# Attention probabilities turned by VectorE and DRAM instead of TensorE, with value products 7 units behind the scores

## The chip, the cores and the metric

One core of one Trainium2 chip runs the whole program. The metric is device time in microseconds for one execution. The engines named below are TensorE (PE, with its weight loads PEld), VectorE (DVE), ScalarE (ACT), GpSimd (POOL) and SyncE (SP, which here only issues transfers). Each engine works through its own list of instructions in order and waits on semaphores. Sixteen DMA engines carry the transfers that SP, GpSimd or ScalarE issue.

## The reference

The reference is one layer of a transformer trunk on 512 tokens of width 2048, all in float32: sliding-window attention, its output projection, a gated embedding and a last norm. What matters here is the attention.

```python
q, k, v, gate = jnp.split(h @ w_in, [...])          # 32 query heads, 4 key and value heads, 64 wide
scores = einsum('bnqhgd,bnjhd->bnhgqj', q, kb) * 64 ** -0.5 + bias   # window of 128 keys, bias by distance
m = maximum(scores.max(-1), sink)
e = exp(scores - m)
probs = e / (e.sum(-1) + exp(sink - m))
out = einsum('bnhgqj,bnjhd->bnqhgd', probs, vb)
return (out * silu(gate)) @ w_out
```

Each query sees itself and the 127 tokens before it. Softmax runs along the keys, and the product with the values sums over the keys. A matmul sums over partitions, so the probabilities, which come out of softmax with queries on the partitions and keys along the row, must be turned before that product.

## The kernel before

**Precision.** A float32 number is split into a high part in the fast float32r format and the rest. A product is three matmuls, high by high, low by high and high by low (`mm3`, lines 123 to 128, so most TensorE time in the profile stands on lines 126 to 128). Each weight tile of 128 x 1024 is loaded (line 102, SP), copied to its high part by ScalarE (line 109) and its low part is made by VectorE (line 110). Three raw buffers go round: a load waits until the tile three before it has been split.

**Stages.** First the norm and the first projections (to about 74 us). Then the attention stage: 30 column blocks of queries (`qps`) and gates (`gps`) are still to be projected, 16 groups of `mm3` each, and the attention's small products go in between. Then the output projection, and then the gated embedding, which ends with the store. The two last stages use a scheme that multiplies sums of weight blocks. Those sums are made in DRAM during the attention stage: SP issues copies (line 723) and GpSimd issues transfers that add a second block (line 725). Each copy and each add is 512 KB, 64 of each, paced by `sums_in`.

**Units.** The attention has 64 units: 8 groups of four heads (`TWOS`, index `d`) by 8 stretches of 64 queries (`UNITS`, index `g`). A unit has 2 x 128 rows: 4 heads by 32 queries, twice. `scores(i)` issues the score products (line 485), bias additions and the maximum on VectorE (lines 513 to 525), the exponential on ScalarE (line 529), the reciprocal of the sum (line 531), and the scaling by it into a tile `pr` (line 542). Where a unit lies at an odd place, the two halves of its keys are swapped on the way, so that rows of keys line up with the values.

`turn(i)` turns `pr` on TensorE by a product with the identity (line 551, into a PSUM bank `pt`), and ScalarE and VectorE split the result into high and low (lines 564 and 565; a group's first unit, `g == 0`, has only 64 keys and its own form, lines 558 to 562). From `g == 2` on, GpSimd selects a triangle of the result into `own` (line 575), and ScalarE copies the upper or the lower half of that (line 585). `weigh(i)` makes the products with the values (lines 601 to 605), and each second unit adds both halves into `U` (lines 614 to 616, with two temporary tiles). Later `gate_value` (line 630) multiplies `U` by the gate, which frees the `U` tile.

**Order.** TensorE, SP, VectorE, ScalarE and GpSimd keep the program's order in this stage; no planner changes it. The loop at lines 936 to 973 writes that order: iteration `i` issues the first part of `scores(i)`, `turn(i - 2)` and `weigh(i - 3)`, then some 7 groups of the projection, with the rest of the small work placed between the groups by their number `n` (`some(W.todo)` makes the next weight tile, `chores` and `idle` hold evacuations of the projections and gates). It has 67 iterations, and `left // (blocks + 2 - i)` deals out the groups. `q_at` (line 181) fixes which of the 30 column blocks are queries, so that each group of heads has its queries in time.

**A turn by DRAM that is there already.** Between the output projection and the next stage, `turn_blocks` (lines 1062 to 1075) has VectorE turn 32 x 32 blocks, GpSimd store them to DRAM and gather them back (lines 1077 to 1083) with the blocks in their turned places.

Of the kernel before, what the change touches and what calls it, by code (L numbers as in the profile page):

```python
# [11 lines left out]
F32 = mybir.dt.float32  # L12
# [7 lines left out]
S = 512  # L20
P = 128
# [5 lines left out]
PAIRS = HEADS // 2  # L27
# [28 lines left out]
def trunk_kernel(ctx: ExitStack, tc: tile.TileContext, a: dict):  # L56
# [292 lines left out]
    for part in (first_q[0][0], first_q[1][0], *first_q[0][1:], *first_q[1][1:]):  # L349
        part()  # L350

    kt = [kvq.tile([P, S], F32, name=f"kt{t}") for t in range(2)]
    K = {}

    def make_key(h):
# [113 lines left out]
    def scores(i):  # L469

        d, g = divmod(i, UNITS)
        if g == 4 and d + 1 < TWOS:
            load_bias(d + 1)
        of_keys = K[d // 2].rearrange("p j l k -> p (j l k)")

        s_ps = spsum.tile([P, 2, S], F32, tag="w", name=f"s{i}")  # L480
        number = [min(2 * g + u + 1, 5) * QB for u in range(2)]
        for u in range(2):
            first, n = max(2 * g + u - 4, 0), number[u]
            st = Q[d][:, 2 * g + u].rearrange("p h q -> p (h q)")
# [24 lines left out]
        bias = biases[d][:, ::-1]  # L509
        if g < 2:  # L510
            for u, n in enumerate(number):
                blocks_of, high, low = by_block(t[:, u, 1 : 1 + n], u, n)
                nc.vector.tensor_add(blocks_of, high, bias[:, KEYS - n :].rearrange("p (j k) -> p j k", k=QB))
            for u, n in enumerate(number):
                blocks_of, high, low = by_block(t[:, u, 1 : 1 + n], u, n)
                nc.vector.tensor_add(blocks_of, low, blocks_of)
        else:
            x = t[:, :, 1 : 1 + KEYS].rearrange("p u (j k) -> p u j k", k=QB)
            of = s_ps[:, :, : 2 * KEYS].rearrange("p u (j l k) -> p u l j k", l=2, k=QB)
            spread = bias.rearrange("p (j k) -> p j k", k=QB).unsqueeze(1).to_broadcast([P, 2, KEYS // QB, QB])  # L520
            nc.vector.tensor_add(x, of[:, :, 0], spread)
            nc.vector.tensor_add(x, of[:, :, 1], x)
# [12 lines left out]
        for u in range(2):  # L535
            out, src = T[i][:, u], pr[u]
            if g == 0:
                out = T[i][:, 0, u * HB : (u + 1) * HB]
            if late and (g + u) % 2:
                out = out.rearrange("p (h k) -> p h k", h=2)[:, ::-1]  # L540
                src = src.rearrange("p (h k) -> p h k", h=2)
            nc.scalar.mul(out, src, sm[:, 4 + u : 5 + u])

    def turn(i):


        d, g = divmod(i, UNITS)
        pr = T.pop(i)
        pt = bank(f"pt{i}", "t")[:, :256]
        for u in range(2 if g else 1):  # L550
            nc.tensor.transpose(pt[:, u * P : (u + 1) * P], pr[:, u, :], ident)  # L551

        r = operands.tile([P, 2, 256], F32R, tag="r", name=f"r{i}", bufs=2)
        rh, rl = (r[:, l].rearrange("p (h u q) -> p u h q", h=4, u=2) for l in range(2))
        src = pt.rearrange("p (u h q) -> p u h q", u=2, h=4)
        if g == 0:
            lower, upper = slice(0, HB), slice(HB, P)
            nc.scalar.copy(rh[lower, 0], src[lower, 0])
            nc.scalar.copy(rl[upper, 1], src[upper, 0])
            nc.vector.tensor_sub(rh[upper, 0], src[lower, 0], rh[lower, 0].bitcast(F32))  # L560
            nc.vector.tensor_sub(rh[upper, 1], src[upper, 0], rl[upper, 1].bitcast(F32))
            nc.scalar.copy(rh[lower, 1], rl[upper, 1].bitcast(F32))
        else:
            nc.scalar.copy(rh, src)  # L564
            nc.vector.tensor_sub(rl, src, rh.bitcast(F32))  # L565
        yield
# [20 lines left out]
    def weigh(i):  # L587
# [3 lines left out]
        kv = d // 2  # L591
        r, own = PT.pop(i)
        if g == 0:
            U[d] = apool.tile([P, 2, S], F32, tag="u", name=f"u{d}", bufs=3)
# [14 lines left out]
        if b:  # L609
            dst = U[d][:, :, n * P : (n + 1) * P].rearrange("p u (b q) -> p b u q", b=2)  # L610
            lower, upper = slice(0, 64), slice(64, 128)
            tmp = [apool.tile([P, 2, 2, HB], F32, tag=f"tmp{e}", name=f"tmp{e}_{i}", bufs=1) for e in range(2)]
            for e, (o, x) in enumerate(((lower, upper), (upper, lower))):
                nc.scalar.copy(tmp[e][o], ops[x, :, :, e, :])
            for e, o in enumerate((lower, upper)):
                nc.vector.tensor_add(dst[o], ops[o, :, :, e, :], tmp[e][o])
        if g == UNITS - 1:
            for c in (2 * d, 2 * d + 1):
                weighed.add(c)
# [299 lines left out]
    def sums_in(i):  # L919


        if i == 0:
            return range(0, SUMS_EARLY, 2)
        if i < 4:
            return range(4 * i + 3, min(4 * i + 7, SUMS_EARLY), 2)
        n, of = SUM_STEPS - SUMS_EARLY, blocks - 4
        return range(SUMS_EARLY + (i - 4) * n // of, SUMS_EARLY + (i - 3) * n // of)

    left = KC * (len(kinds) - 1)
# [3 lines left out]
            of.pop(0)()  # L933

    softmax = iter(())
    for i in range(blocks + 3):

        before, softmax = softmax, scores(i) if i < blocks else iter(())
        turned = turn(i - 2) if 2 <= i < blocks + 2 else iter(())
        value = weigh(i - 3) if 3 <= i else iter(())  # L940
        next(turned, None)
        next(value, None)
        next(softmax, None)
        next(turned, None)
        next(before, None)
        next(softmax, None)
        first_chores(i, 0)
        if i in (6, 20, 36):
            idle.extend(make_key(1 + i // 16))
        todo = left // (blocks + 2 - i) if i < blocks + 2 else 0  # L950
        left -= todo
        for n in range(max(todo, 6)):
            if n < todo:
                next(proj)
            if n == 0:
                first_chores(i, 1)
                some(W.todo)
                some(chores or idle)
            elif n == 2:
                next(turned, None)  # L960
                next(value, None)
                if len(chores) > 1:
                    some(chores)
            elif n == 3:
                next(softmax, None)
            elif n == 4:
                first_chores(i, 2)
                some(chores or idle)
            elif n == 5:
                next(softmax, None)  # L970
        if i < blocks:
            for n in sums_in(i):
                sum_weights(n)
    for _ in proj:
# [863 lines left out]
```

## Time and profile before

| | |
|---|---|
| Median of 3 runs | 781.91 us (781.47 to 781.96) |
| Profiled execution | 781.41 us, span 779.7 us |
| TensorE busy | 770.1 us, 99% of the span |
| VectorE busy | 618.9 us, 79% |
| ScalarE busy | 529.3 us, 68% |
| GpSimd busy | 169.8 us, 22% |
| DMA | 217.22 MB, mean 279 GB/s |
| Granted TensorE clock | 0.997 |

The page gives the busy time of each engine and its share of the span, then the span in 40 equal slices, where each digit is a share in tenths. The queues q1 and q0 are the transfers issued by SP and those issued by GpSimd. A group of instructions is a line of the kernel, an engine, an operation, the tiles it writes and reads, a shape and a count, then the total busy time and the mean of one in ns, and then the idle time before them with what ended it. In a table of stretches each row has the stretch, its length, the busy time and number of instructions of each engine, the granted clock, the share of time in which the DMA engines were busy, and the GB/s that they moved. That share is a sum over packets, and can pass 1 where two packets overlap on an engine.

### The profile page before, as it was taken

Reading aid. Unit: us, or ns where it says so; the run is one execution under the profiler, and the core shown is the slowest. Engines: PE = TensorE matmul, PEld = TensorE weight load, DVE = VectorE, ACT = ScalarE, POOL = GpSimd, SP = SyncE. Lnnn points to the kernel's source line nnn. Section 1 sums busy time; section 2 is a strip of 40 time slices with the busy share of each in tenths; the row PEclk is TensorE's granted clock in tenths of the full one; section 3 lists DMA queues with packets and bytes.
Section 4 is the critical chain, followed back from the end, with each engine's and each line's share of the span. In section 5 each row is a group of like instructions: output and inputs, shape, how many; then the busy total and the mean of one; then the engine's idle time right before and its main releaser. Section 6 shows DMA issues by size and latency. Waiting matters only on the chain.

```text
span 779.7 us, 11154 instructions
## 1 busy us (share of the span) xinstructions
PE 770.1 (99%) x3652; PEld 644.1 (83%) x3652; DVE 618.9 (79%) x1069; ACT 529.3 (68%) x1121; POOL 169.8 (22%) x307
## 2 busy tenths in 40 slices
PE   9999999999999999999999999999999999999995
PEld 8888888888888888888888888888888888888884
DVE  4546697876978688777877799968799889999995
ACT  6743586766777676766766664577766888867874
POOL 0201523132232313132332200112101122221111
PEclk9999999999999999999999999999999999999998
DMA  9978899999999999999998588999899999999956
GB/s 343 305 207 301 182 260 311 272 312 258 287 247 278 280 241 278 277 279 277 248 288 218 136 298 313 359 290 290 318 389 337 320 284 295 325 264 309 321 132 216
DMA packets 52858, 217.22 MB, mean 279 GB/s; under 512 B 8112, under 2 KB 9136, under 8 KB 46720
## 3 DMA queue, kind: packets, MB, share of 16 engines
q1 hardware_dynamic: 39280, 156.67, 56.5%
q0 software_dynamic: 13520, 59.83, 36.2%
q8 instruction: 29, 0.48, 0.3%
q14 instruction: 29, 0.24, 0.1%
HBM read 199.65 MB, written 82.89 MB: 362 GB/s over the span
## 4 chain that ended last, share of the span: by engine, by line
PE 98%; issue 1%; DVE 0%; POOL 0%; POOLq 0%; DVEq 0%
PE gps L126 7%; PE gps L127 7%; PE gps L128 7%; PE qps L126 7%; PE qps L128 7%; PE qps L127 7%; PE o L126 6%; PE o L127 6%; PE o L128 6%; PE g L127 5%; PE g L128 5%; PE g L126 5%; PE s L485 2%; PE vps L290 2%; PE o L603 2%; PE pt L551 2%
## 5 line engine op out<-in xcount | busy, mean ns | idle before, releaser
L766 DVE TENSOR_TENSOR blo<-braw,bhi 128x1024 fp32r<-128x1024 f32 x100 | 121.5, 1220 | 20.9 <-ACT bhi L765 19.9
L765 ACT CAST bhi<-braw 128x1024 fp32r<-128x1024 f32 x100 | 105.1, 1052 | 47.1 <-PE o L128 15.1
L126 PE MATMUL gps<-xh,whi 128*128 128x512 f32 x256 | 100.0, 390 | 0.0
L127 PE MATMUL gps<-xl,whi 128*128 128x512 f32 x256 | 99.9, 390 | 0.0
L128 PE MATMUL gps<-xh,wlo 128*128 128x512 f32 x256 | 99.8, 390 | 0.0
L126 PE MATMUL qps<-xh,whi 128*128 128x512 f32 x224 | 87.8, 392 | 0.0
L128 PE MATMUL qps<-xh,wlo 128*128 128x512 f32 x224 | 87.5, 390 | 0.0
L127 PE MATMUL qps<-xl,whi 128*128 128x512 f32 x224 | 87.4, 390 | 0.0
L575 POOL TENSOR_SCALAR_AFFINE_SELECT own<-r 64x512 fp32r<-64x512 f32 (+1 forms) x48 | 32.5, 677 | 238.4 <-DVE r L565 234.4
L110 DVE TENSOR_TENSOR wlo<-wraw,whi 128x1024 fp32r<-128x1024 f32 x60 | 73.5, 1227 | 2.8 <-ACT whi L109 2.7
L126 PE MATMUL o<-bhi,fho 128*128 128x512 f32 x192 | 74.8, 390 | 0.0
L127 PE MATMUL o<-blo,fho 128*128 128x512 f32 x192 | 74.7, 389 | 0.0
L128 PE MATMUL o<-bhi,flo 128*128 128x512 f32 x192 | 74.7, 389 | 0.0
L109 ACT CAST whi<-wraw 128x1024 fp32r<-128x1024 f32 x60 | 62.3, 1040 | 4.6 <-issue 4.1
L126 PE MATMUL g<-bhi,fhg 128*128 128x512 f32 x160 | 62.3, 390 | 0.0
L127 PE MATMUL g<-blo,fhg 128*128 128x512 f32 x160 | 62.2, 389 | 0.0
L128 PE MATMUL g<-bhi,flg 128*128 128x512 f32 x160 | 62.2, 389 | 0.0
L128 PEld LDWEIGHTS gps<-xh,wlo 128*128 128x128 f32 x256 | 48.1, 188 | 10.3
L126 PEld LDWEIGHTS gps<-xh,whi 128*128 128x128 f32 x256 | 48.1, 188 | 9.2
L529 ACT ACTIVATE t<-t,sm 128x129 f32<-128x129 f32 (+1 forms) x128 | 49.6, 389 | 8.7 <-DVE sm L525 7.4
L127 PEld LDWEIGHTS gps<-xl,whi 128*128 128x128 f32 x256 | 48.1, 188 | 8.9
L565 DVE TENSOR_TENSOR r<-pt,r 128x256 fp32r<-128x256 f32 x56 | 23.7, 424 | 38.9 <-ACT r L564 38.1
(299 smaller groups left out, 1827.6 us busy)
## 6 DMA issues: line engine op xcount, KB each, us to landing
wraw<-in_w_gate_in SPq DMA_DIRECT2D x32, 512.0 KB, 8.1
w_out<-in_w_out POOLq DMA_DIRECT2D x32, 512.0 KB, 9.1
braw<-w_out SPq DMA_DIRECT2D x32, 512.0 KB, 8.1
wraw<-in_w_q SPq DMA_DIRECT2D x28, 512.0 KB, 6.7
braw<-in_w_out SPq DMA_DIRECT2D x22, 512.0 KB, 5.7
braw<-in_ple_gate SPq DMA_DIRECT2D x22, 512.0 KB, 6.9
ple_gate<-in_ple_gate POOLq DMA_DIRECT2D x20, 512.0 KB, 8.9
xw<-in_first SPq DMA_DIRECT2D x14, 640.5 KB, 6.5
```

Of the source, the lines that this page charges most:

```text
L109: nc.scalar.copy(hi, raw)
L110: nc.vector.tensor_sub(lo, raw, hi.bitcast(F32))
L126: nc.tensor.matmul(ps, sh, mh, start=first, stop=False, skip_group_check=more)
L127: nc.tensor.matmul(ps, sh, ml, start=False, stop=False, skip_group_check=more)
L128: nc.tensor.matmul(ps, sl, mh, start=False, stop=last, skip_group_check=more)
L290: nc.tensor.matmul(v_ps[t], h[:, c], part_of(high_at, 256, 512), start=f, stop=e, skip_group_check=True)
L485: nc.tensor.matmul(s_ps[:, u, : 2 * n], st, of_keys[:, first * 2 * QB : (first * QB + n) * 2], start=True, stop=True)
L529: nc.scalar.activation(su, su, AF.Exp, bias=sm[:, u : u + 1], accum_out=sm[:, 2 + u : 3 + u])
L565: nc.vector.tensor_sub(rl, src, rh.bitcast(F32))
L575: nc.gpsimd.affine_select(out=flat(own), in_=flat(r).bitcast(F32), pattern=[[0, 8], [sign, HB]], compare_op=ALU.is_ge, fill=0.0, base=-HB ...
L765: nc.scalar.copy(hi[:, :n], raw)
L766: nc.vector.tensor_sub(lo[:, :n], raw, hi[:, :n].bitcast(F32))
```

## The change

`turn` no longer uses TensorE. ScalarE scales the probabilities in place. VectorE turns each 32 x 32 block of a unit into one half of a tile `turned`, which holds two units. `send` (issued by ScalarE) stores that tile to DRAM, and `fetch` (four transfers issued by SP, one for each 32 keys) gathers it into a tile `back`, where keys are on the partitions. `turn` splits from `back` instead of from PSUM. A fourth of the pairs begin with a unit of 64 keys, and leave out the unused quarter (`within`).

Iteration `i` now does `scores(i)`, the split of unit `i - 5`, and the value products of unit `i - 7`, in 70 iterations over which the projection's groups are dealt evenly. A pair `a` is stored in iteration `2a + 2` after group 4 and gathered in iteration `2a + 4` after group 2; its first unit is split in iteration `2a + 5` after group 2. The adds into weight sums go on for four iterations more. `q_at` follows the new pace. To make room, `U` has two buffers instead of three, and the seventh `U` lies where the keys were (`both_kt`), and one temporary tile takes the place of two.

```diff
-    q_at = {int(0.5 + 3.516 * (c // 2)) - 3 + c % 2: c for c in range(2, PAIRS)}
+    q_at = {int(0.5 + 3.333 * (c // 2)) - 3 + c % 2: c for c in range(2, PAIRS)}
...
-        T[i] = operands.tile([P, 2, P], F32, tag="pr", name=f"pr{i}", bufs=3)
         for u in range(2):
-            out, src = T[i][:, u], pr[u]
+            nc.scalar.mul(pr[u], pr[u], sm[:, 4 + u : 5 + u])
+        yield
+
+        a, v = divmod(i, 2)
+        if not v:
+            T[a] = operands.tile([P, 512], F32, tag="turned", name=f"turned{a}", bufs=2)
+        to = T[a].rearrange("p (j v u q) -> p v u j q", j=4, v=2, u=2)[:, v]
+        for u in range(2):
+            out, src = to[:, u], pr[u].rearrange("p (j q) -> p j q", q=QB)
             if g == 0:
-                out = T[i][:, 0, u * HB : (u + 1) * HB]
+                out = to[:, 1, 2 * u : 2 * u + 2]
             if late and (g + u) % 2:
...
-            nc.scalar.mul(out, src, sm[:, 4 + u : 5 + u])
+                out = out[:, ::-1]
+            nc.vector.transpose(out, src)
+
+    def within(v, a):
+        return v[:, :, QB if a % (UNITS // 2) == 0 else 0 :]
+
+    def send(a):
+        apart_of[a] = tc.dram_tile([P, 512], F32, name=f"turned_of{a}")
+        nc.scalar.dma_start(*(within(v.rearrange("p (j x) -> p j x", j=4), a) for v in (apart_of[a], T.pop(a))))
+
+    def fetch(a):
+        back[a] = operands.tile([P, 512], F32, tag="back", name=f"back{a}", bufs=2)
+        src = apart_of.pop(a).rearrange("(h k) (j x) -> j k h x", h=4, j=4)
+        for j in range(4):
+            to = back[a][QB * j : QB * j + QB].rearrange("p (h x) -> p h x", h=4)
+            nc.sync.dma_start(within(to, a), within(src[j], a))
 
     def turn(i):
-        pr = T.pop(i)
-        pt = bank(f"pt{i}", "t")[:, :256]
-        for u in range(2 if g else 1):
-            nc.tensor.transpose(pt[:, u * P : (u + 1) * P], pr[:, u, :], ident)
+        src = back[a].rearrange("p (h v x) -> p v h x", h=4, v=2)[:, v]
...
-        n, of = SUM_STEPS - SUMS_EARLY, blocks - 4
+        n, of = SUM_STEPS - SUMS_EARLY, blocks
...
-    for i in range(blocks + 3):
+    total = left
+    turned = iter(())
+    for i in range(blocks + 7):
         before, softmax = softmax, scores(i) if i < blocks else iter(())
-        turned = turn(i - 2) if 2 <= i < blocks + 2 else iter(())
-        value = weigh(i - 3) if 3 <= i else iter(())
-        next(turned, None)
+        value = weigh(i - 7) if 7 <= i else iter(())
         next(value, None)
         next(softmax, None)
         next(turned, None)
         next(before, None)
         next(softmax, None)
...
-        todo = left // (blocks + 2 - i) if i < blocks + 2 else 0
-        left -= todo
-        for n in range(max(todo, 6)):
+        share = total * (i + 1) // (blocks + 6) - total * i // (blocks + 6) if i < blocks + 6 else 0
+        for n in range(max(share, 6)):
...
+            if n == 4 and i % 2 == 0 and 2 <= i <= blocks:
+                send(i // 2 - 1)
+            if n == 2 and i % 2 == 0 and 4 <= i <= blocks + 2:
+                fetch(i // 2 - 2)
+            if n == 2:
+                next(turned, None)
+            if n == 1:
+                next(before, None)
...
+            if n == 2:
+                turned = turn(i - 5) if 5 <= i < blocks + 5 else iter(())
                 next(turned, None)
...
-        if i < blocks:
+        if i < blocks + 4:
             for n in sums_in(i):
                 sum_weights(n)
```

More of the change, by code (lines that the diff above doesn't have):

```diff
@@ L350, in trunk_kernel @@
         part()
-    kt = [kvq.tile([P, S], F32, name=f"kt{t}") for t in range(2)]
+    both_kt = kvq.tile([P, 2, S], F32, name="kt")
+    kt = [both_kt[:, t] for t in range(2)]
     K = {}
@@ L553, in turn @@
+    def turn(i):
+        g = i % UNITS
+        a, v = divmod(i, 2)
+        src = back[a].rearrange("p (h v x) -> p v h x", h=4, v=2)[:, v]
         r = operands.tile([P, 2, 256], F32R, tag="r", name=f"r{i}", bufs=2)
[L554 to L555 removed]
         if g == 0:
+            rh, rl = (r[:, l].rearrange("p (h u q) -> p u h q", h=4, u=2) for l in range(2))
+            src = src[:, :, QB:]
@@ L557, in turn @@
             lower, upper = slice(0, HB), slice(HB, P)
[L558 to L561, printed above, removed]
+            nc.scalar.copy(rh[lower, 0], src[lower])
+            nc.scalar.copy(rl[upper, 1], src[upper])
+            nc.vector.tensor_sub(rh[upper, 0], src[lower], rh[lower, 0].bitcast(F32))
@@ L562, in turn @@
+            nc.vector.tensor_sub(rh[upper, 1], src[upper], rl[upper, 1].bitcast(F32))
             nc.scalar.copy(rh[lower, 1], rl[upper, 1].bitcast(F32))
         else:
+            rh, rl = (r[:, l].rearrange("p (h x) -> p h x", h=4) for l in range(2))
             nc.scalar.copy(rh, src)
@@ L593, in weigh @@
         if g == 0:
-            U[d] = apool.tile([P, 2, S], F32, tag="u", name=f"u{d}", bufs=3)
+            U[d] = both_kt if d == 6 else apool.tile([P, 2, S], F32, tag="u", name=f"u{d}", bufs=2)
         if b == 0:
@@ L611, in weigh @@
             lower, upper = slice(0, 64), slice(64, 128)
-            tmp = [apool.tile([P, 2, 2, HB], F32, tag=f"tmp{e}", name=f"tmp{e}_{i}", bufs=1) for e in range(2)]
+            tmp = apool.tile([P, 2, 2, HB], F32, tag="tmp", name=f"tmp_{i}", bufs=1)
             for e, (o, x) in enumerate(((lower, upper), (upper, lower))):
-                nc.scalar.copy(tmp[e][o], ops[x, :, :, e, :])
+                nc.scalar.copy(tmp[o], ops[x, :, :, e, :])
             for e, o in enumerate((lower, upper)):
-                nc.vector.tensor_add(dst[o], ops[o, :, :, e, :], tmp[e][o])
+                nc.vector.tensor_add(dst[o], ops[o, :, :, e, :], tmp[o])
         if g == UNITS - 1:
```

30 lines of the change are left out of this document (14 added, 16 removed).

## The prediction

> **What bounds the kernel now.** First the page: busy times, slices, DMA queues, chain.
>
> ```profile
> span 779.7 us, 11154 instructions
> PE 770.1 (99%) x3652; PEld 644.1 (83%) x3652; DVE 618.9 (79%) x1069; ACT 529.3 (68%) x1121; POOL 169.8 (22%) x307
> ...
> DMA  9978899999999999999998588999899999999956
> ...
> q1 hardware_dynamic: 39280, 156.67, 56.5%
> q0 software_dynamic: 13520, 59.83, 36.2%
> ...
> PE 98%; issue 1%; DVE 0%; POOL 0%; POOLq 0%; DVEq 0%
> ```
>
> TensorE is busy through the whole span and is 98% of the chain. So a TensorE instruction taken away is time gained, as long as nothing else is as full. The slice row of DMA says that something is: nine tenths or more nearly throughout. Next, the stretches. The attention stage runs from its first score product (81.5) to the first product of the output stage (450.3).
>
> ```profile
> core 0: us, PE busy (x) PEld busy (x) DVE busy (x) ACT busy (x) POOL busy (x), PEclk, DMA share, GB/s
> 81.50:450.30 368.80, 368.80 (x1809) 309.64 (x1809) 286.11 (x633) 252.76 (x695) 101.75 (x190) 1.00 0.94 261
> 110.00:190.00 80.00, 80.00 (x394) 67.17 (x394) 60.74 (x139) 56.11 (x154) 23.70 (x45) 1.00 1.02 296
> 300.00:330.00 30.00, 30.00 (x147) 25.12 (x147) 22.86 (x54) 21.52 (x61) 9.12 (x18) 1.00 1.02 295
> 410.00:450.00 40.00, 40.00 (x197) 33.55 (x196) 31.70 (x61) 26.53 (x67) 8.44 (x13) 1.00 0.68 181
> 450.00:640.00 190.00, 190.00 (x849) 157.56 (x848) 165.60 (x201) 130.81 (x192) 28.54 (x47) 1.00 0.96 320
> ```
>
> TensorE never stops in the stage and its clock is whole. The DMA engines are at 0.94 on average, and in two long stretches at 1.02, where they move 295 and 296 GB/s. I read that rate as their full rate for this mix of weight loads, copies and accumulating sums. Only the last 40 us are loose (0.68).
>
> **What the change removes.** The transposes by TensorE, 120 of them:
>
> ```profile
> L551 PE MATMUL pt<-ident,pr 128*128 128x128 f32 x120 | 23.4, 271 | 0.0
> ```
>
> Matmuls overlap, so 271 ns is not their price. Two visits of the attention to TensorE differ in them alone:
>
> ```profile
> 443.91 0.38 PE L551 MATMUL pt<-ident,pr 128*128 128x128 f32 x2
> 444.04 0.48 PE L603 MATMUL o<-r,V 128*128 128x256 f32 x2
> 444.36 0.28 PE L605 MATMUL o<-own,DV 128*128 128x256 f32 x1
> 444.48 0.40 PE L126 MATMUL gps<-xh,whi 128*128 128x512 f32 x1
> ...
> 449.95 0.40 PE L603 MATMUL o<-r,V 128*128 128x256 f32 x2
> 450.18 0.28 PE L605 MATMUL o<-own,DV 128*128 128x256 f32 x1
> 450.30 0.40 PE L126 MATMUL o<-bhi,fho 128*128 128x512 f32 x1
> ```
>
> With a pair of transposes the visit takes 444.48 - 443.91 = 0.57 us, without it 450.30 - 449.95 = 0.35. A pair costs 0.22 us; 56 units have a pair, 8 have one: 56 x 0.22 + 8 x 0.11 = **13.2 us**. On TensorE's account the stage falls from 368.8 to 355.6 us. The projection products and their number stay (between the two visits eight groups of three take 449.95 - 444.48 = 5.47, so 0.68 each); they are dealt over 70 iterations, so one lasts 355.6 / 70 = 5.08 us on average.
>
> The Trainium skill, VectorE: DVE Perf Modes, The three transpose paths, speaks against the change: a full 128x128 transpose belongs on TensorE if PSUM will do as its destination, since VectorE turns only 32x32 blocks; it gives 390 and 311 ns in bf16. By its 390 ns the removed work would be an estimated 47 us; the two visits above show 13.2, and they decide.
>
> **What it adds on the engines.** VectorE turns two 128x128 tiles in a unit, 128 instructions. A wider one exists later in the kernel:
>
> ```profile
> L1073 DVE STREAM_TRANSPOSE blocks<-x1s x8: 672/704/705, 574.2 to 626.6; 128x512 f32<-128x512 f32 x8
> L110 DVE TENSOR_TENSOR wlo<-wraw,whi 128x1024 fp32r<-128x1024 f32 x60 | 73.5, 1227 | 2.8 <-ACT whi L109 2.7
> L522 DVE TENSOR_TENSOR t<-s,t 128x320 f32<-128x320 f32 x48 | 23.6, 492 | 1.7
> L565 DVE TENSOR_TENSOR r<-pt,r 128x256 fp32r<-128x256 f32 x56 | 23.7, 424 | 38.9 <-ACT r L564 38.1
> L560 DVE TENSOR_TENSOR r<-pt,r 64x128 fp32r<-64x128 f32 x8 | 2.3, 284 | 14.7 <-ACT r L559 14.7
> ```
>
> From L110 and L522 VectorE takes 1.04 ns a column and about 0.16 us beside it; 704 ns for 512 columns fits. So 128 columns cost 0.30 us (a quarter of 704, 0.18, is the lower bound), 64 columns 0.22: 112 x 0.30 + 16 x 0.22 = 37 us (23 at the least). VectorE's load becomes 286.1 + 37 = 323 us in 355.6, **91%** after 78%. It fits if its waits shrink: it idles 368.8 - 286.1 = 82.7 us now, of which 38.9 + 14.7 lie before L565 and L560, which wait through ScalarE for TensorE's transposes and will wait for data asked for an iteration before. I cost it at nothing; the cover is VectorE's other idle time, and if it goes, the score additions come late and with them the next score products. Splitting from SBUF instead of PSUM I leave at its price (L110 reads SBUF and L565 PSUM along one line).
>
> ScalarE issues 32 stores, SP 128 gathers (four for each pair of units):
>
> ```profile
> L102 SPq DMA_DIRECT2D wraw<-in_w_gate_in x32: 327/334/572, 48.2 to 419.4; - x32
> DMA to landing us min/median/max: 3.5/7.3/18.6
> ...
> SPq L102 <- DVE wlo L110: 219.8, 47, 10.9
> ```
>
> At 0.33 us an issue that is 11 us on ScalarE ((252.8 + 11) / 355.6 = 74%) and 42 on SP, which now waits 220 us for free weight buffers. Both hidden. A store waits on ScalarE for VectorE's turned blocks, which stand three steps before it (about 2 us); behind it are that iteration's splits. A gather waits on SP for the store to land; behind it are the next weight load, the next copy and bias loads. Weight loads have landed as late as 18.6 us without TensorE stopping, so this alone costs nothing. Keys' room reused for one U and one tmp tile instead of two: their former readers are done iterations before; nothing. The rescheduled q tiles (3.333) still come four iterations ahead; nothing.
>
> **What it adds on the DMA engines.** This is the term that decides. A pair of units is 128 x 512 floats, 262 KB, once out and once back; every fourth pair leaves out a quarter. 30 full pairs x 2 x 262 KB = 15.7 MB.
>
> Present load: 261 GB/s x 368.8 us = 96.3 MB, at the full rate of 296 GB/s 325 us. The price of the new 15.7 MB is not in the trace; it is bounded by the two queues of the page. q1 moves 156.67 MB in 56.5% of 779.7 us, 356 GB/s: 44 us. Store at that rate and gathers (pieces of 512 bytes) at that of q0, 59.83 MB in 36.2%, 212 GB/s: 22 + 37 = 59 us. I take 48 (22 and 26): nothing accumulates, so the gathers are nearer q1, but their pieces are smaller than its typical 4 KB packets (156.67 MB / 39280).
>
> Together 325 + 48 = 373 us of full-rate DMA, in a stage that TensorE would end after 355.6. The excess of 17 us can in part be queued. In 110 to 190 the engines moved (296 - 261) x 80 = 2.8 MB above the average, 9.5 us of work that had been queued while TensorE never waited. The last store, gathers and sums stand at iterations 64 to 67. So: up to iteration 66 the engines must move 373 less the three or four weight loads still to come (524 KB each at 296, 6 us) less 9.5 = 357.5 us; four iterations without scores at 4.9 us follow (19.6). **Stage 377 us, 8 more than now.** With 44 it is 373, with 59 388. The profiled execution took 781.4 us (span 779.7 and 1.7 around it; median shown 781.9), so 789.7; I say **789**.
>
> The Trainium skill, DMA: Bandwidth & Descriptors, Issuing engines are not separate DMA queues, says the same of the store on ScalarE's queue: it runs on the same 16 engines and saves only issue time. Had it engines of its own, the sum would be 22 us less and the stage TensorE's 355.6.
>
> **The rivals.**
>
> *The DMA engines take it (faster).* If 296 GB/s is what is asked for and not what they can do, TensorE keeps its pace: 781.4 - 13.2 = 768. For it: 320 GB/s in the output stage at 0.96 only, the slack in 410 to 450, and sums dealt over four more iterations, which fills it. Against it: a share of 1.02 in both stretches. If a third of the excess remains, 775.
>
> *The round trip is too long (slower).* From a store (iteration 2a+2, step 4) to the split of what came back (2a+5, step 2) ScalarE has three iterations less two groups: 15.2 - 1.4 = 13.9 us. Behind it there is this margin before the product:
>
> ```profile
> 206.56 0.40 ACT L585 CAST own<-own 64x256 fp32r<-64x256 f32 x1
> ...
> 209.04 0.28 PE L605 MATMUL o<-own,DV 128*128 128x256 f32 x1
> ```
>
> 209.04 - 206.96 = 2.1 us. Less four issues (1.3), 14.7 us. The trace's own store and gather by DRAM, in the later stage:
>
> ```profile
> L1075 POOL DMA_DIRECT2D apart<-blocks x4: 561/561/561, 576.4 to 628.0; - x4
> ...
> DMA to landing us min/median/max: 5.2/8.5/10.7
> ...
> L1083 POOL DMA_DIRECT2D s<-apart x24: 552/552/579, 557.0 to 639.2; - x24
> ...
> DMA to landing us min/median/max: 3.8/7.1/8.8
> ```
>
> 8.5 + 7.1 = 15.6 us, 0.9 late, 0.3 an iteration: 64 x 0.3 = 19 us, 787, hardly to be told from the forecast but by its place. With latencies 2 us longer it is 1.0 an iteration: 832 by the arithmetic, less in fact, since a slower stage loads the engines less; I put 805. Against it: medians of another queue and of bigger stores.
>
> *VectorE becomes the bound (slower).* If its waits stay as they are, 323 + 83 = 406 us, 819; it decides from idle time above 33 us on. Against it: two thirds of that idle time had a cause that goes.
>
> *Nothing measurable.* The queue drains better or the gathers cost 40: stage 368 to 370, 782.
>
> **How the numbers follow.** Forecast (DMA-bound, 785 to 798) 0.44; the long round trip 0.10 (800 to 815); VectorE 0.04; DMA takes it 0.34 (768 to 780); nothing 0.08. Within 0.2% (780.3 to 783.5) is about what a measurement here can't tell from no change. Faster 0.34, same 0.08, slower 0.58. The range leaves out the ends of both sides: 769 to 803; the forecast's own is 784 to 798 (44 to 59 us of transfers).
>
> **What would show it.** Right: TensorE idle in the stage, after waits that end in a landing (weights, or the gathered tile in ScalarE's split), a DMA share at or over 1.0 from 100 to 430, landings of weights well over 7.3 us, stage about 377. The visit to TensorE should have shrunk by 0.22 us, VectorE's turn should take 0.30. Wrong: TensorE without gaps and a stage of 356 (the engines had room); gaps with a DMA share under 0.97 (round trip or VectorE, told apart by who is waited for). A price of the gathers outside 22 to 37 us in total moves the sum by that much.

## The result, and the profile after

| | before | after |
|---|---|---|
| Median | 781.9 us (781.47 to 781.96) | 844.35 us (837.77 to 845.30) |
| Ratio, 95% interval | | 1.0782 (1.0727 to 1.0837) |
| Profiled execution, span | 781.4, 779.7 us | 844.2, 842.4 us |
| Attention stage, to the first output product | 368.8 us | 430.4 us |

The change makes the kernel slower by 62.4 us. The forecast was 789 us (769 to 803): right in its sign, 55 us short. All times are medians; one of the four executions of the kernel with GpSimd's gathers (section 5), 853.10 us, fell into a slower state of the chip, and that kernel's numbers stand without it (its median with it is 843.49). The lines of the page of the changed kernel that answer to those of before:

```profile
span 842.4 us, 11457 instructions
PE 784.0 (93%) x3532; PEld 648.3 (77%) x3532; DVE 644.0 (76%) x1197; ACT 531.9 (63%) x1121; POOL 163.1 (19%) x307
...
DMA  8987999999899999998999996999989999999965
...
q1 hardware_dynamic: 57712, 164.55, 56.3%
q0 software_dynamic: 13520, 59.83, 34.0%
q10 hardware_dynamic: 7680, 7.87, 2.7%
...
PE 52%; DMA 27%; DVE 8%; ACT 6%; issue 3%; SPq 2%; ACTq 0%; DVEq 0%; POOL 0%; POOLq 0%
DMA wraw<-in_w_gate_in 9%; DMA turned_of<-turned 7%; DMA back<-turned_of 5%; PE o L127 5%; PE o L126 5%; PE o L128 5%; DMA wraw<-in_w_q 5%; PE g L127 4%; PE g L128 4%; PE g L126 4%; ACT whi L109 2%; PE qps L126 2%; PE qps L127 2%; PE qps L128 2%; PE vps L290 2%
```

The chain, 98% TensorE before, is now half TensorE, and a quarter of it is transfers of three kinds: weights (9% and 5%), the store (7%) and the gather (5%). Its stretches, with the columns as before:

```profile
core 0: us, PE busy (x) PEld busy (x) DVE busy (x) ACT busy (x) POOL busy (x), PEclk, DMA share, GB/s
81.50:511.90 430.40, 382.62 (x1690) 314.16 (x1689) 310.99 (x760) 255.85 (x695) 96.29 (x191) 0.95 0.95 259
110.00:190.00 80.00, 70.78 (x307) 58.35 (x306) 57.42 (x145) 48.48 (x134) 15.95 (x35) 0.91 0.99 281
190.00:300.00 110.00, 95.60 (x429) 78.22 (x428) 81.68 (x203) 65.58 (x182) 25.87 (x53) 0.97 0.94 260
```

Of the span's 62.7 us more, 61.6 lie in this stage. TensorE now idles 430.4 - 382.6 = 47.8 us there. Its busy time should have fallen to 355.6 and rose to 382.6, at a granted clock of 0.95. The DMA engines, at 0.95, are not full over the whole stage. Who waits for whom, first the engines, then SP's queue (total us, times, longest):

```profile
PEld o L630 <- ACT own L610: 28.3, 17, 3.9
PE o L630 <- ACT own L610: 24.8, 15, 3.7
ACT r L582 <- DMA back<-turned_of: 21.8, 5, 6.9
ACT r L589 <- DMA back<-turned_of: 18.6, 6, 6.2
ACT whi L109 <- DMA wraw<-in_w_gate_in: 14.7, 5, 6.9
...
SPq L569 <- DMA turned_of<-turned: 162.3, 23, 13.9
```

ScalarE's split (lines 582 and 589) waits 40.4 us for the gathered tile, and TensorE's product of the values (line 630) waits for ScalarE. SP, which waited 219.8 us for free weight buffers before, now waits 162.3 us in front of the gathers for stores to land. One such round trip in the timeline, first of SP, then of ScalarE, then of TensorE (start, duration, instruction, idle time before it in brackets):

```profile
232.57 0.52 SPq L102 DMA_DIRECT2D wraw<-in_w_gate_in  x1
245.20 1.80 SPq L569 DMA_DIRECT2D back<-turned_of  x4
247.10 0.47 SPq L748 DMA_DIRECT2D w_out<-w_out  x1
247.67 0.53 SPq L102 DMA_DIRECT2D wraw<-in_w_gate_in  x1
...
248.51 0.40 ACT L610 CAST own<-own 64x256 fp32r<-64x256 f32 x1
255.15 0.40 ACT L589 CAST r<-back 128x256 fp32r<-128x256 f32 x1 [6.23 <-DMA back<-turned_of]
...
255.60 0.85 PE L628 MATMUL o<-r,V 128*128 128x256 f32 x2 [1.20 <-ACT r L589]
259.77 0.58 PE L630 MATMUL o<-own,DV 128*128 128x256 f32 x1 [3.32 <-ACT own L610]
```

SP issues nothing from 233.09 to 245.20, when the store landed. The gather then takes until 255.05, and ScalarE stands still for 6.23 us. The next weight load stands behind the gather on SP and goes out at 247.67.

### The profile page after: what moved, and what is told of

Its sections match the earlier page's. It is cut to its first block, busy times and chain, and to the rows that moved or that the text cites. A ratio compares the mean times of both kernels' runs of the same rounds, so it can differ in the third digit from the quotient of the medians.

```text
span 842.4 us, 11457 instructions
## 1 busy us (share of the span) xinstructions
PE 784.0 (93%) x3532; PEld 648.3 (77%) x3532; DVE 644.0 (76%) x1197; ACT 531.9 (63%) x1121; POOL 163.1 (19%) x307
## 4 chain that ended last, share of the span: by engine, by line
PE 52%; DMA 27%; DVE 8%; ACT 6%; issue 3%; SPq 2%; ACTq 0%; DVEq 0%; POOL 0%; POOLq 0%
DMA wraw<-in_w_gate_in 9%; DMA turned_of<-turned 7%; DMA back<-turned_of 5%; PE o L127 5%; PE o L126 5%; PE o L128 5%; DMA wraw<-in_w_q 5%; PE g L127 4%; PE g L128 4%; PE g L126 4%; ACT whi L109 2%; PE qps L126 2%; PE qps L127 2%; PE qps L128 2%; PE vps L290 2%
## 5 line engine op out<-in xcount | busy, mean ns | idle before, releaser
L127 PE MATMUL gps<-xl,whi 128*128 128x512 f32 x256 | 102.5, 401 | 0.0
L126 PE MATMUL gps<-xh,whi 128*128 128x512 f32 x256 | 102.4, 400 | 0.0
L128 PE MATMUL gps<-xh,wlo 128*128 128x512 f32 x256 | 102.0, 398 | 0.1
L126 PE MATMUL qps<-xh,whi 128*128 128x512 f32 x224 | 92.3, 412 | 0.0
L127 PE MATMUL qps<-xl,whi 128*128 128x512 f32 x224 | 91.6, 409 | 0.0
L128 PE MATMUL qps<-xh,wlo 128*128 128x512 f32 x224 | 90.9, 406 | 0.0
L536 ACT ACTIVATE t<-t,sm 128x128 f32<-128x128 f32 (+1 forms) x128 | 43.6, 389 | 66.4 <-DVE sm L532 50.1
L109 ACT CAST whi<-wraw 128x1024 fp32r<-128x1024 f32 x60 | 62.2, 1038 | 32.5 <-DMA wraw<-in_w_gate_in 14.7
L126 PEld LDWEIGHTS gps<-xh,whi 128*128 128x128 f32 x256 | 49.8, 195 | 9.5
L128 PEld LDWEIGHTS qps<-xh,wlo 128*128 128x128 f32 x224 | 44.6, 199 | 10.0
```

What stands on the lines that cost most here:

```text
L109: nc.scalar.copy(hi, raw)
L126: nc.tensor.matmul(ps, sh, mh, start=first, stop=False, skip_group_check=more)
L127: nc.tensor.matmul(ps, sh, ml, start=False, stop=False, skip_group_check=more)
L128: nc.tensor.matmul(ps, sl, mh, start=False, stop=last, skip_group_check=more)
L536: nc.scalar.mul(pr[u], pr[u], sm[:, 4 + u : 5 + u])
```

## The experiments

Two ideas had to be told apart; each expectation puts numbers on its own form of them. *Volume*: the DMA engines have less room than the forecast gave them. *Round trip*: the wait of a gather for its store costs time by itself.

**1. The wait for the store, taken away.** The gathers read an earlier pair's store.

```diff
-        src = apart_of.pop(a).rearrange("(h k) (j x) -> j k h x", h=4, j=4)
+        of = a if a < 2 else a - 1 if a % 4 == 2 else a - 2
+        src = apart_of[of].rearrange("(h k) (j x) -> j k h x", h=4, j=4)
```

> The changed kernel, but each gather reads what an earlier pair stored (one or two pairs before), so SP need not wait for the store just issued; the values of the wrong pair are used, all transfers and all other waits stay. Theory A (the 16 DMA engines are full, as forecast): same bytes, so 838 to 848 us. Theory B (the round trip: SP stands still at the gather until the store lands, and weight loads and copies stand behind it): SP's 162 us of waiting go, stage near the forecast's DMA sum, 775 to 800 us. Theory C (VectorE is the bound): 838 to 848.

Measured 820.44 us (818.95 to 821.11), 1.0489 (1.0474 to 1.0505), between the numbers of the theories. So the wait costs 844.35 - 820.44 = 23.9 us, and 38.5 remain without it. SP's 162.3 us in front of the gathers shrink to 39.3, so the edit takes away most of the wait and not all of it. Its stage, and what is left of SP's wait:

```profile
81.50:487.39 405.89, 374.12 (x1690) 309.38 (x1689) 312.58 (x762) 255.46 (x695) 96.33 (x191) 0.96 0.99 275
...
SPq L570 <- DMA turned_of<-turned: 39.3, 8, 11.0
```

Now the DMA engines are full from end to end (0.99), at 275 GB/s and not 296.

**2. No transfers at all.** The split reads the turned tile itself; `turned` has four buffers.

```diff
-                send(i // 2 - 1)
+                pass
...
-                fetch(i // 2 - 2)
+                back[i // 2 - 2] = T.pop(i // 2 - 2)
```

> The changed kernel without the store and the gathers: the split reads the turned tile itself, whose blocks do not stand where they should (this part of the turn is left out). Four turned tiles instead of two, since they live longer. Theories A and B: nothing is left to wait for, TensorE sets the pace, 781.4 - 13.2 = 768, at most 774. Theory C: VectorE has all its work still, 800 us or more.

Measured 775.05 us (773.91 to 776.51), 0.9913 (0.9898 to 0.9928), 1 us over the most that theories A and B allowed and far from C's 800. Its stage:

```profile
81.50:443.83 362.33, 357.55 (x1690) 299.46 (x1688) 310.93 (x762) 254.91 (x695) 96.26 (x190) 1.00 0.96 265
```

VectorE's turns are in it, at 310.93 us in 362.33, and TensorE idles 4.8 us: VectorE is not the bound. TensorE's 1690 matmuls take 357.55 us where the forecast had 355.6. The changed kernel has the same 1690 at 382.62, so 25.1 us of its stage are the same work drawn out, at a granted clock of 0.95.

**3. The new order with the old turn.** TensorE turns, and the split, the products, `q_at` and the dealing are those of the change. No transfers; `pr` has six buffers.

```diff
-            nc.vector.transpose(out, src)
+            nc.scalar.mul(out, src, sm[:, 4 + u : 5 + u])
...
+        for u in range(2 if g else 1):
+            nc.tensor.transpose(pt[:, u * P : (u + 1) * P], pr[:, u, :], ident)
```

> The new order (split of unit i-5, values of unit i-7, 70 iterations, same rooms for U and tmp) with the old turn by TensorE and no transfers for it; six pr tiles. Theories A, B, C: the order itself costs nothing, 779 to 785 us as before. If the order is part of the loss: 790 or more.

Measured 789.75 us (789.36 to 791.02), 1.0105 (1.0088 to 1.0122): the order alone costs 7.8 us, which the forecast had at nothing, and so had the three theories. Between this run and the last only the turn differs: 789.75 - 775.05 = 14.7 us, for 13.2 forecast. Where the 7.8 us are:

```profile
110.00:190.00 80.00, 76.91 (x369) 63.66 (x368) 60.25 (x137) 54.61 (x154) 18.04 (x39) 0.98 0.95 280
81.50:458.18 376.68, 373.59 (x1813) 311.10 (x1812) 287.29 (x635) 253.20 (x695) 97.83 (x191) 1.00 0.94 256
```

The idle 3.1 us all lie in 110 to 190, and 4.8 us are busy time (373.59 against 368.80 before). Some 1.7 of these are the clock, which the trace has at 0.50 from 119.4 to 122.8; why TensorE is busy longer for the rest isn't settled.

**4. The traffic alone, added to the kernel before.** The same 32 stores and 128 gathers, of a tile that nobody needs; `U` and the keys share room as in the change. Then the stores alone, then the gathers alone.

```diff
+    def send(a):
+        idle_of[a] = tc.dram_tile([P, 512], F32, name=f"idle_of{a}")
+        nc.scalar.dma_start(*(within(v.rearrange("p (j x) -> p j x", j=4), a) for v in (idle_of[a], idle_src)))
+    def fetch(a):
+        idle_back[a] = operands.tile([P, 512], F32, tag="back", name=f"idle_back{a}", bufs=1)
...
+            if n == 4 and i % 2 == 0 and 2 <= i <= blocks:
+                send(i // 2 - 1)
+            if n == 2 and i % 2 == 0 and 4 <= i <= blocks + 2:
+                fetch(i // 2 - 2)
```

> The kernel before with the same 32 stores (ScalarE's queue) and 128 gathers (SP's queue) at the same places of the order, of a tile of zeros; nobody reads what comes back, and a gather reads an earlier store, so it does not wait for the one just issued. U and the keys share room as in the change. Theory A in its strong form (the bytes explain the loss): 825 to 850 us. The forecast's sum (325 + 48 us of full-rate work in a stage of 369): 786 to 800. Theory B: 780 to 792, since no result hangs on the transfers.

> The kernel before with the 32 idle stores alone, no gathers. Theory A2: 347 + 23 at 0.99: stage 373, 786 us. If it is the number of transfers and not their time that counts: a fifth of the 32.5 us of both, 788. If a third queue disturbs the weight loads by itself: over 795.

> The kernel before with the 128 idle gathers alone (they read two tiles stored at the start). Theory A2: 347 + 32 at 0.99: stage 383, 796 us. If SP's 128 issues in front of weight loads are what costs: 805 to 815, nearly all of the 32.5 us.

Measured 814.49 us (809.39 to 819.05), 1.0414 (1.0367 to 1.0462), for both; 786.10 (784.00 to 788.93), 1.006 (1.0041 to 1.008), for the stores; 789.94 (788.29 to 790.98), 1.0103 (1.0087 to 1.0118), for the gathers. So 4.3 and 8.1 us each alone (786 and 796 were expected), and 32.5 together, which lies between the forms of its expectation and meets none. The run with both, its stage and its queues, and q1 of the run with the gathers alone:

```profile
81.50:484.37 402.87, 382.33 (x1813) 315.87 (x1812) 285.86 (x633) 253.49 (x695) 99.14 (x191) 0.98 0.99 278
...
q1 hardware_dynamic: 57712, 164.55, 58.1%
q0 software_dynamic: 13520, 59.83, 34.3%
q10 hardware_dynamic: 7680, 7.87, 2.8%
...
q1 hardware_dynamic: 57712, 164.55, 59.6%
```

The prices can now be read off its span of 813.7 us. The stores have a queue of their own: 2.8% x 813.7 = 22.8 us. The gathers are what q1 has more than before: 58.1% x 813.7 - 56.5% x 779.7 = 32 us. The engines' time of the stage before is its share, 0.94 x 368.8 = 347 us. Together 347 + 55 = 402 us in a stage of 402.9, which is the share of 0.99 over again: they are full. It also fits that the parts don't add. A stage of 368.8 us has 22 us to spare: the stores' 22.8 pass that by 1 us (4.3 measured), the gathers, 29 when alone (59.6% x 787.5 - 56.5% x 779.7), by 7 (8.1 measured), and both by 33 (32.5 measured). This is the volume theory, and run 1 ends on nearly the same stage (405.9).

How the full engines stop TensorE is seen in the waits of the run with both:

```profile
ACT r L584 <- DMA idle_back<-idle_of: 27.2, 7, 6.3
...
PE o L625 <- ACT own L605: 12.4, 9, 6.5
```

Nobody reads `idle_back`. ScalarE stands 27.2 us before its split because a store in front of it can't be issued until a gather of SP's has landed (section 6 says why), and TensorE's product of the values waits for ScalarE behind it. So this run holds a second cost beside the volume, and it too needs stores and gathers together. The two aren't told apart: that the engines are at 0.99 leaves little for shorter waits to give, but a run without these waits is missing.

The Trainium skill, DMA: Bandwidth & Descriptors, Issuing engines are not separate DMA queues, fits this trace: the stores that ScalarE issues (q10) take 2.8% of the time of the same 16 engines, and they add 814.49 - 789.94 = 24.6 us to the gathers, though the wait just shown has a part in that.

**5. The round trip: more distance, and another queue for the gathers.** First the gathers one iteration later, and the split and the products two (`turn(i - 7)`, `weigh(i - 9)`, 72 iterations).

```diff
-            if n == 2 and i % 2 == 0 and 4 <= i <= blocks + 2:
-                fetch(i // 2 - 2)
+            if n == 2 and i % 2 and 5 <= i <= blocks + 3:
+                fetch((i - 5) // 2)
```

> The changed kernel with the round trip given more room: gathers one iteration later in SP's list (2a+5), split of unit i-7, values of unit i-9, 72 iterations; every wait is real and the result is whole. Theory A2 (DMA time, sized by the run with idle traffic: 347 us of it in the stage before, 55 more, at a share of 0.99): stage 406, 819 us. Theory B (the wait for the store adds 24 us on top): the same 815 to 822, since SP no longer meets a store in flight; if it is not the wait that adds them, 840 to 848.

Then the changed kernel with GpSimd as the issuer.

```diff
-            nc.sync.dma_start(within(to, a), within(src[j], a))
+            nc.gpsimd.dma_start(within(to, a), within(src[j], a))
```

> The changed kernel, with the gathers issued by GpSimd instead of SP: the same transfers, the same wait of a gather for its store, but SP no longer stands still in front of a gather with the next weight loads behind it. Theory 1 (the 24 us that the wait for the store costs, 844.4 against 820.4, are SP standing still in front of it: SP waits 162.3 us for the stores): about 820, and the waits of ScalarE for the weight tile are gone. Theory 2 (the 24 us are the round trip itself, the split of a pair comes before its gather has landed): 840 to 850, and ScalarE's waits for the gathered tile stay at 40 us. Beside either, GpSimd's own queue of weight copies now stands behind the gathers; if that decides, over 850.

Measured 837.56 us (835.79 to 840.01), 1.0716 (1.0694 to 1.0738), and 840.48 (837.14 to 846.49), 1.0761 (1.0707 to 1.0816). The first falls between the numbers of its two theories; neither gives back much of the 23.9 us. The waits say why. With more distance:

```profile
ACT whi L109 <- DMA wraw<-in_w_gate_in: 40.8, 12, 7.6
ACT whi L109 <- DMA wraw<-in_w_q: 25.8, 11, 8.5
...
SPq L569 <- DVE r L590: 62.0, 16, 6.6
SPq L569 <- DVE sm L532: 37.2, 10, 6.5
```

With GpSimd:

```profile
SPq L102 <- DVE wlo L110: 236.8, 42, 14.9
...
ACT r L589 <- DMA back<-turned_of: 43.0, 13, 6.8
ACT own L610 <- POOL own L600: 21.6, 10, 6.2
```

In the first the gathered tile is in time, but SP still stands in front of a gather (now, by the row with line 590, for a free `back`, which VectorE's split releases), and ScalarE waits 66.6 us for weights that were issued late. In the second SP is free again (it waits for weight buffers, as before the change), but the tile is late by 43 us in all. So both theories of that expectation hold, each for one half. The two edits together:

> The two edits that gained little alone, together: the gathers one visit-pair later and the split and the products two blocks later (as in the run with the lag of 9, 837.6), and the gathers issued by GpSimd (as in the run with GpSimd, 843.5). In the first SP still stood in front of the gathers with the weight loads behind them (for the buffers of back, 56 us, and for the weights' copies ScalarE then waited 66 us); in the second SP was free, but ScalarE waited 43 us for the gathered tile. Theory 1 and 2 are then two halves of one cost, each hidden behind the other: with both gone the kernel falls to what the DMA engines take, (0.94 x 368.8 + 55) / 0.99 = 406 us in the stage, 820. Theory 3 (the queues of GpSimd: its own products of the values, 151 us busy in this stage with the gathers against 86, now stand behind gathers that wait; ScalarE waited 21.6 us for them): 835 to 845, with ScalarE's waits for own grown.

Measured 825.77 us (822.23 to 827.63), 1.0543 (1.051 to 1.0576), between the theories' numbers. That is 18.6 of the 23.9 us: the wait for the store acts in two ways, by a late tile and by weight loads held behind it on SP, and taking away one uncovers the other. What is left over 820.4:

```profile
ACT own L610 <- POOL own L600: 18.4, 11, 2.9
...
PE o L630 <- ACT own L610: 25.2, 14, 4.0
```

GpSimd's triangle (line 600) stands behind the gathers that it issues, which theory 3 said. That these waits are the remaining 5 us is argued, not shown. The engines' share in this stage is 0.94, so here it isn't their time alone that bounds.

**6. The number of transfers.** First no DRAM: 16 gathers of 16 KB for each pair straight from `turned`, all issued by SP.

```diff
-        src = apart_of.pop(a).rearrange("(h k) (j x) -> j k h x", h=4, j=4)
+        of = T.pop(a).rearrange("p (j x) -> p j x", j=4)
...
-            nc.sync.dma_start(within(to, a), within(src[j], a))
+            for h in range(4):
+                nc.sync.dma_start(within(to[:, h : h + 1], a), within(of[QB * h : QB * h + QB, j : j + 1], a))
```

> The changed kernel without the DRAM tile: no store, and each pair is gathered from the turned tile in SBUF by 16 transfers of 32 rows (SP), issued in iteration 2a+3. Half the bytes and no store to wait for; the result is whole. Theory A2: 347 + 32 us (the gathers' time with idle traffic) at 0.99: stage 383, 796 us. Theory B alone (waits, not bytes): about 775, as without DRAM, plus what 512 issues on SP cost.

Measured 979.98 us (976.65 to 982.56), 1.2533 (1.2503 to 1.2564). Neither theory came near. Half the added bytes, no round trip, and it is the slowest run. Its waits, and its gathers on SP (the shortest, median and longest issue in ns):

```profile
ACT whi L109 <- DMA wraw<-in_w_gate_in: 100.9, 17, 12.2
ACT whi L109 <- DMA wraw<-in_w_q: 89.3, 15, 11.9
...
SPq L570 <- DMA wraw<-in_w_gate_in: 38.5, 26, 3.0
...
L570 SPq DMA_DIRECT2D back<-turned x512: 507/588/1163, 94.9 to 628.4; - x171
```

The issues alone keep SP busy for some 512 x 0.588 = 301 us of the stage's 566, where the forecast had 0.33 us for one, and every weight load stands behind up to 16 of them. Besides, a gather on SP (line 570) waits for weight loads of SP's own to land, which it does not read. How much of the time each of the two explains isn't shown; the engines' share is only 0.72. The second suggested a limit on the transfers under way, and so the next two: the regrouping moved to the store, so that four stores of 64 KB by ScalarE go with one gather of 256 KB, issued by SP or by GpSimd.

```diff
-        nc.scalar.dma_start(*(within(v.rearrange("p (j x) -> p j x", j=4), a) for v in (apart_of[a], T.pop(a))))
+        rows = apart_of[a].rearrange("(j k) (h x) -> h k j x", j=4, h=4)
+        src = T.pop(a).rearrange("p (j x) -> p j x", j=4)
+        for h in range(4):
+            nc.scalar.dma_start(within(rows[h], a), within(src[QB * h : QB * h + QB], a))
...
-            nc.sync.dma_start(within(to, a), within(src[j], a))
+        to, src = (v.rearrange("p (h x) -> p h x", h=4) for v in (back[a], apart_of.pop(a)))
+        nc.sync.dma_start(within(to, a), within(src, a))
```

> The changed kernel, with the regrouping moved from the gather to the store: ScalarE issues four stores of 64 KB in pieces of 512 bytes, and SP one gather of 256 KB in rows of 2 KB. The same bytes and the same number of pieces; SP's queue carries one transfer for a pair instead of four. Counted from the traces, at no issue of SP are more than 7 of its earlier transfers still on their way, in any of the kernels so far. Theory S (SP's queue holds 8 transfers at most, and the small gathers fill it, so the weight loads behind them start late; idle stores alone cost 4.3 us and idle gathers alone 8.1, both 32.5): the 20 us that were not additive go, about 820 to 825. Theory D (the time of the DMA engines alone decides, 22.8 + 32.3 us in whichever order): 840 to 846.

> Both edits together: one gather of 256 KB for a pair, issued by GpSimd, the regrouping in four stores. If SP's standing still (24 us) and its full queue (20 us) are two separate costs, 844 - 44 = 800. If only the first is real, 820. If the DMA engines' time and the round trip decide, 840 or more.

Measured 887.67 us (885.84 to 890.93), 1.1358 (1.1332 to 1.1384), and 860.98 (858.18 to 862.46), 1.1011 (1.0983 to 1.1038). The first went the wrong way, past both numbers expected of it. The second, which differs in GpSimd's issuing the gather, is 26.7 us better than the first, but not than the changed kernel, as the last of its three cases had it (840 or more). In the first the timeline of ScalarE has

```profile
263.99 12.49 ACTq L564 DMA_DIRECT2D turned_of<-turned  x4
276.54 0.69 ACT L536 ACTIVATE t<-t,sm 128x128 f32<-128x128 f32 x2 [12.95 <-DMA wraw<-in_w_gate_in]
```

ScalarE, with the softmax behind it, stands 12.95 us in the middle of issuing a store, until a weight load lands that SP issued. The trace's records say how the two are tied. All transfers of SP and ScalarE signal their landing on the same eight semaphores, taken in turn, and those of GpSimd on eight others. An issue waits until the transfer that used its semaphore before has landed: none of the issues counted below started earlier. Each semaphore is thus a slot for one transfer. Counted over the issues of SP and ScalarE from 81.5 to 450 us, as far as the records have their landing:

```
kernel                          issues   most earlier ones under way   issues with all seven others under way
before                             154   7                              17
after                              280   7                              60
gathers without the wait (1)       295   7                             126
idle stores and gathers (4)        287   7                             129
16 gathers of 16 KB (6)            447   7                             143
four stores, one gather (6)        253   7                              35
```

Never more than eight at once, in any kernel. This is a property of the program, which has eight semaphores there, and not of the queue: the Trainium skill, DMA: Bandwidth & Descriptors, Why a DMA increments its semaphore by 16 and not by 1, asks for one semaphore for each transfer in flight, because a count shared by two can pass before the first has fully landed. It means that ScalarE's small store queues for a slot with SP's 512 KB loads, and that a gather waiting in SP's line for a store keeps the slots behind it unused. What more semaphores would give wasn't tried. In the changed kernel itself the limit is a part of the waits at most: 23 of the 32 groups of gathers were issued within 0.1 us of their store's landing, not of a slot coming free.

## Why the prediction was right or wrong

**Removed from TensorE, 13.2 us: right.** 14.7 between runs 2 and 3, and in run 2 357.6 us of TensorE in the stage for 355.6.

**VectorE's turns at no cost: right.** Each takes 0.20 to 0.31 us, where 0.22 and 0.30 were forecast, and run 2 rejects VectorE as the bound:

```profile
L550 DVE STREAM_TRANSPOSE turned<-t x128: 202/273/314, 89.6 to 487.7; 128x128 f32<-128x128 f32 x112, 128x64 f32<-128x64 f32 x16
```

**The DMA engines decide: right for the larger part, the 38.5 us that run 1 keeps (slots may share in them); their present load, 325 us: wrong.** This is the first step that failed. I took bytes over the highest rate seen, 96.3 MB at 296 GB/s. The row quoted beside it gave the load directly, a share of 0.94 of 368.8 us: 347. The 296 GB/s were the rate of a stretch whose share passed 1; over a whole stage the engines moved 275 to 278 at 0.99 (runs 1 and 4). The error is 22 us.

**New transfers, 48 us: mis-sized.** The stores took 22.8 for 22. The gathers, in pieces of 512 bytes, took 32 for 26; the bounds, 22 to 37, held. (By the forecast's own sum its bounds of 44 and 59 us for both give 786 and 801 us, not the 784 or 785 and 798 that it states.) With 347 + 55 in the forecast's own sum, less the same 6 and 9.5 and with the same 19.6, the stage is 406 and the time 819; run 1 has 405.9 and 820.4. These two terms are nearly the whole distance from 789 to run 1; whether the credit and the tail were each right isn't shown by that.

**"So this alone costs nothing", of the gathers on SP: wrong.** This is the second step that failed. The argument compared one late load (18.6 us) with buffers that were then in time. Here SP stood still 23 times, up to 13.9 us, with every later weight load behind it, and with most of that wait gone the kernel is 23.9 us faster (run 1).

**The long round trip as a rival: its place was right, and it comes on top.** The forecast had 8.5 + 7.1 = 15.6 us against a margin of 14.7, in place of the DMA limit, at 805 and with a chance of 0.10. From a store's issue to the landing of its last gather the changed kernel takes 16.5 us on average (8 to 23), and 22 of 32 take over 14.7. It was priced as an alternative to the DMA limit, but the two go together: in run 1, with the engines at 0.99, a group of gathers takes 10.5 us on average from issue to landing, and here at 0.95 it takes 7.7, both more than the 7.1 of the forecast. They had to be added; the 24 us between 820 and 844 are known from run 1 alone, and the forecast's rows gave no price for them.

**The order at no cost: wrong by 7.8 us** (run 3). Whether it still costs anything where the DMA engines bound isn't shown. **The two cheerful cases** (DMA takes it, 768; nothing, 782) fall with run 4, whose traffic alone costs 32.5 us.

**What would show it.** The landings of weights were to be well over 7.3 us; their median is 8.2, only a little over:

```profile
DMA to landing us min/median/max: 3.8/8.2/15.4
```

A share at or over 1.0 from 100 to 430 didn't come either (0.99 and 0.94 in the two stretches above). The sign that did tell was the one put down for the round trip or VectorE, gaps at a share under 0.97 (0.95 over the stage).

## What to carry to other kernels

Take the load of the DMA engines from their share of time in the stage, not from bytes over the best rate; what is left of the stage is the whole room for new transfers, and here what went past it was paid nearly in full (33 us reckoned, 32.5 measured). A round trip by DRAM through a queue that also carries loads can cost twice: its consumer waits for the tile, and whatever stands behind the gather in that queue starts late; mending one uncovers the other. Count transfers as well as bytes, since issuers that share completion semaphores share their slots, and a small store can then hold up a compute engine.

## What the runs showed of the hardware

TensorE's clock falls to half for some microseconds after short waits. In the changed kernel the waits of TensorE for the values are 3.9 us at the longest, and the granted clock is 0.91 from 110 to 190 and 0.95 over the stage. There the same matmuls took 25.1 us more than in run 2, at 1.00. The trace has ten stretches at half clock in the stage, each 3.4 or 6.8 us long, 44 us in all, which lose 22 of the 25.1 us. One of them, with the wait before it (in the row of the stretch the third number from the end is the clock):

```profile
180.29 0.39 PE L630 MATMUL o<-own,DV 128*128 128x256 f32 x1 [1.77 <-ACT own L610]
...
181.20:184.60 3.40, 3.40 (x10) 2.61 (x9) 3.32 (x12) 1.52 (x8) 1.18 (x2) 0.50 1.04 310
```

And a longer wait after which it stayed whole:

```profile
301.82 0.39 PE L630 MATMUL o<-own,DV 128*128 128x256 f32 x1 [2.97 <-ACT own L610]
...
301.82:317.20 15.38, 15.38 (x73) 12.89 (x73) 10.20 (x25) 8.62 (x23) 4.88 (x9) 1.00 0.98 221
```

So the length of one wait doesn't decide it, and what does isn't shown. The Trainium skill, TensorE: Matmul & The Clock Gate, HAM oscillation, warns of idle gaps over about 3.4 us; here the clock fell after one of 1.77, and the measurement decides. A stall can therefore cost more than its own length (3.4 us at half clock lose 1.7), which no term of the forecast held.
